# Layer 1 attention: gated outputs kept on chip in places that keys and weights leave, its pools in another order, and gate matmuls packed into the first head

## The chip, the cores and the metric

One core of one Trainium2 chip. The metric is device time in microseconds (us) of one execution of the whole program. The core has TensorE (PE in the profile, with PEld for its weight loads), VectorE (DVE), ScalarE (ACT), GpSimd (POOL) and SyncE (SP); in this kernel SP issues every DMA, in order.

## The reference

A trunk of two layers on x of 2048 tokens by 1024 features, float32. Layer 0 is windowed and chunked attention with a gate; the change leaves it alone. Layer 1 is differential attention with 8 heads of two 64-wide halves, causal by chunks of 64 tokens:

```python
q, k, v, gate = jnp.split(rms_norm(x, norm_g) @ w_in, [C_QK, 2 * C_QK, 2 * C_QK + C_W], axis=-1)
# per head: q1, q2 and k1, k2 are the normed, rotated halves
p1 = jax.nn.softmax(jnp.where(mask, s1, NEG_INF), axis=-1)
p2 = jax.nn.softmax(jnp.where(mask, s2, NEG_INF), axis=-1)
a = p1 - lam * p2
o = jnp.einsum('bhqk,bkhd->bqhd', a.astype(v.dtype), v)
o = rms_norm(o, subln_g) * (1.0 - lambda_init)
y = (o.reshape(b, s, C_W) * jax.nn.silu(gate)) @ w_out
return x + y
```

## The kernel before

All of it is float32, with operands split into a high and a low part (names ending in H and L), so that a product of the dense kind is three matmuls (`mm3`, L212 to L216: aH·bH, aH·bL, aL·bH). Call three such matmuls of 512 columns a unit.

Layer 0 and the projection of layer 1 (`project(1)`, which leaves q, k, v in DRAM) come first. The attention of layer 1 is `_mix1`. It goes over four blocks of 512 tokens from the last (b = 3) to the first (b = 0), and in each over 8 heads. A block b attends to b + 1 blocks of keys. Three streams are woven into one order by a function `pace`, when the program is built:

- **Scores** (`heads`, `scores`): for each head SP loads b + 1 blocks of keys (`load`, tiles k0 and k1, one for each half, tags with 4 buffers each; tiles vH and vL, 4 buffers each) and the queries (qd, ql, 2 buffers). For each of 4 rows of 128 tokens, each half and each 512 keys: two matmuls (L865, L866) into one of 4 PSUM banks, a maximum on DVE (L869) and an exponential on ACT (L872). Then POOL (every fifth time DVE) scales and adds the two halves (L893 to L899).
- **Values** (`values`): some way behind the scores (LAG1 units), the combined rows are transposed (L912), split (ACT L915, DVE L916) and multiplied with V (L919 to L921); then `gate` normalizes, multiplies with the gate g read back from DRAM, and its second half `rest` ends at L950 with the gated output o of one head and block.
- **Side work** (`side`): the gate projection (`gates`, 4 blocks of 64 units plus a store each 8, 288 steps), and then for each block the output projection (`projected`, 64 units plus 8 steps). Side units are what TensorE does where scores and values wait for the other engines.

How far the side work may be at each point is read from a table, `STAGES1`: pairs of (score units done, side steps done), with straight lines between. A head of block 3 has 58 score units, of block 2 42, of block 1 26, of block 0 10; in all there are 1088. What the table leaves at 1088 is done at the end, in the tail.

The output projection of a block needs the gated outputs of all eight heads as 16 tiles (yH and yL). Before, block 3's are split at once (`split`: ACT L967, POOL L968) and kept in pool `y` (16 buffers). Those of blocks 2 and 1 are stored to a DRAM tensor `o1` (L954), and `fetch` reads them back (tile oy, L978) and splits them when the projection of the block ahead is done, so that one set of 16 buffers serves three blocks in turn. Block 0's go into tiles that keys, values and weights no longer need (list `late`). `projected_last`, for block 0, takes weights for its second half from the places of the last queries and P1, and from k0 and k1.

Tiles share 4 buffers of tag `ot` among gate results, gated outputs, read-back outputs and residual rows.

## Time and profile before

| | us |
|---|---|
| time, median of 3 runs | 2954.62 |
| lowest and highest run | 2950.18, 2968.23 |
| the profiled execution, its own time | 2951.96 |
| span of the profiled execution | 2950.2 |
| mean granted clock of TensorE in it | 0.972 |
| PE, POOL, DVE, ACT busy over the span | 92%, 54%, 65%, 54% |

[...] A row of the view of waits says which engine and line waited for which, for how long in all, how often, and the longest. A row of the timeline gives start, duration, engine, line, operation and, in brackets, the wait ahead of it. The attention of layer 1 runs from about 1840 us to the end at 2950.2 us.

### The profile page before, as it was taken

How to read it: one execution, taken by the hardware profiler on the slowest of the kernel's cores; microseconds unless marked ns; L12 is line 12 of the kernel's file. 1: busy time of each engine (PE TensorE's matmuls, PEld its weight loads, DVE VectorE, ACT ScalarE, POOL GpSimd, SP SyncE). 2: the span in 40 equal slices, each digit the busy share in tenths (PEclk: the TensorE clock that was granted, in tenths of full speed). 3: DMA queues.
4: the chain of work that ended last, by engine and by line, in shares of the span. 5: the costliest groups of instructions: out<-in, count | busy, mean ns of one | idle time of the engine just before them, and what ended most of it. 6: DMA issues, size and time to landing. Idle time of an engine off the chain costs nothing.

```text
span 2950.2 us, 45159 instructions
## 1 busy us (share of the span) xinstructions
PE 2718.6 (92%) x13672; PEld 2242.1 (76%) x13672; DVE 1917.2 (65%) x4652; ACT 1593.5 (54%) x4135; POOL 1604.6 (54%) x1966
## 2 busy tenths in 40 slices
PE   6999999988888889899999998889999999899888
PEld 5888888876777788777788886667777777677667
DVE  7752385266677676498818861665766888878752
ACT  4443543367556565243334331666766777778752
POOL 3541251245345343267745650776777878789851
PEclk9999999999999999999999998999999999999999
DMA  4773343669988886475895455576768777668863
GB/s 149 230 250 120 113 147 120 197 192 249 262 214 212 216 217 170 146 270 197 259 302 191 127 162 158 164 217 197 225 193 234 200 225 214 176 169 243 221 215 114
DMA packets 427537, 580.79 MB, mean 197 GB/s; under 512 B 48160, under 2 KB 198688, under 8 KB 427296
## 3 DMA queue, kind: packets, MB, share of 16 engines
q1 hardware_dynamic: 427296, 577.92, 66.7%
q8 instruction: 109, 1.79, 0.3%
q14 instruction: 132, 1.08, 0.1%
HBM read 413.14 MB, written 164.63 MB: 196 GB/s over the span
## 4 chain that ended last, share of the span: by engine, by line
PE 63%; DMA 15%; DVE 11%; ACT 4%; POOL 3%; issue 3%; SPq 2%; DVEq 0%; ACTq 0%; POOLq 0%
PE p1mm L216 4%; PE p1mm L214 4%; PE p1mm L215 4%; PE p0mm L215 3%; PE p0mm L216 3%; PE p0mm L214 3%; PE cS L865 3%; PE ctr L912 3%; PE cS L866 3%; DMA mks<-bkL 2%; PE cO L920 2%; PE cG L214 2%; PE cG L216 2%; PE com L214 2%; DVE cnm L869 2%
## 5 line engine op out<-in xcount | busy, mean ns | idle before, releaser
L872 ACT ACTIVATE cP<-cS,cnm 128x512 f32<-128x512 f32 (+3 forms) x640 | 399.0, 630 | 173.8 <-DVE cnm L869 96.0
L869 DVE TENSOR_REDUCE cnm<-cS 128x1 f32<-128x512 f32 (+3 forms) x640 | 374.3, 600 | 100.6 <-PE cS L866 95.4
L865 PE MATMUL cS<-ck,cqd 128*128 128x512 f32 (+3 forms) x640 | 262.9, 415 | 60.0 <-ACT cP L872 20.5
L304 POOL TENSOR_TENSOR p0wL<-p0ws,p0wH 128x512 fp32r<-128x512 f32 (+1 forms) x128 | 155.3, 1246 | 276.0 <-ACT p0wH L303 266.4
L216 PE MATMUL p1mm<-p1wH,p1hL 128*128 128x512 f32 x768 | 303.3, 395 | 0.0
L215 PE MATMUL p1mm<-p1wL,p1hH 128*128 128x512 f32 x768 | 302.9, 395 | 0.4 <-POOL p1wL L304 0.4
L214 PE MATMUL p1mm<-p1wH,p1hH 128*128 128x512 f32 x768 | 302.3, 395 | 0.8 <-ACT p1wH L303 0.8
L899 POOL TENSOR_TENSOR cP<-cP,cP 128x512 f32<-128x512 f32 (+3 forms) x256 | 285.2, 1135 | 0.3
L304 POOL TENSOR_TENSOR p1wL<-p1ws,p1wH 128x512 fp32r<-128x512 f32 x128 | 168.0, 1333 | 136.8 <-ACT p1wH L303 97.5
L214 PE MATMUL p0mm<-p0wH,p0hH 128*128 128x512 f32 (+1 forms) x640 | 237.6, 374 | 3.5 <-ACT p0vt L454 2.6
L866 PE MATMUL cS<-ck,cql 128*128 128x512 f32 (+3 forms) x640 | 235.3, 372 | 3.3 <-DMA cql<-qL 3.3
L215 PE MATMUL p0mm<-p0wL,p0hH 128*128 128x512 f32 (+1 forms) x640 | 238.2, 373 | 0.0
L216 PE MATMUL p0mm<-p0wH,p0hL 128*128 128x512 f32 (+1 forms) x640 | 237.7, 372 | 0.1
L916 DVE TENSOR_TENSOR cptL<-ctr,cptH 128x512 fp32r<-128x512 f32 (+1 forms) x320 | 190.7, 599 | 62.4 <-ACT cptH L915 61.4
L865 PEld LDWEIGHTS cS<-ck,cqd 128*128 128x128 f32 x640 | 123.2, 193 | 104.4 <-ACT cP L872 51.2
L915 ACT ACTIVATE cptH<-ctr 128x512 fp32r<-128x512 f32 (+1 forms) x320 | 169.6, 539 | 58.2 <-PE ctr L912 57.0
L893 POOL TENSOR_SCALAR cP<-cP,ccs 128x512 f32<-128x512 f32 (+3 forms) x288 | 191.9, 683 | 0.0
L912 PE MATMUL ctr<-ident,cP 128*128 128x128 f32 x1088 | 175.4, 277 | 1.4 <-POOL cP L899 1.2
L898 POOL TENSOR_SCALAR cP<-cP,ccs 128x512 f32<-128x512 f32 (+3 forms) x256 | 174.0, 693 | 0.0
L214 PEld LDWEIGHTS p1mm<-p1wH,p1hH 128*128 128x128 f32 x768 | 145.3, 189 | 29.9 <-ACT p1wH L303 1.2
L215 PEld LDWEIGHTS p1mm<-p1wL,p1hH 128*128 128x128 f32 x768 | 145.2, 189 | 29.9 <-POOL p1wL L304 0.8
L216 PEld LDWEIGHTS p1mm<-p1wH,p1hL 128*128 128x128 f32 x768 | 145.4, 189 | 29.3 <-issue 0.2
(321 smaller groups left out, 7719.0 us busy)
## 6 DMA issues: line engine op xcount, KB each, us to landing
p1ws<-in_od_w_in_dram SPq DMA_DIRECT2D x56, 512.0 KB, 4.7
p0ws<-in_ev_w_in_dram SPq DMA_DIRECT2D x48, 512.0 KB, 4.3
ck<-kH SPq DMA_DIRECT2D x160, 128.0 KB, 4.0
ck<-kL SPq DMA_DIRECT2D x160, 128.0 KB, 4.2
cvH<-vH SPq DMA_DIRECT2D x80, 256.0 KB, 3.9
cvL<-vL SPq DMA_DIRECT2D x80, 256.0 KB, 4.7
cqd<-qH SPq DMA_DIRECT2D x128, 128.0 KB, 4.9
cql<-qL SPq DMA_DIRECT2D x128, 128.0 KB, 4.7
```

The source lines that it names most:

```text
L214: mm(ps, aH, bH, start=first, stop=False)
L215: mm(ps, aH, bL, start=False, stop=False)
L216: mm(ps, aL, bH, start=False, stop=last)
L304: nc.gpsimd.tensor_tensor(l[:, :width], ws[:, k, :width], f32(h[:, :width]), ALU.subtract)
L865: mm(ps, qd[:, m, js], kt[:, :wd], start=True, stop=False)
L866: self.anchor = mm(ps, ql[:, m, js], kt[:, :wd], start=False, stop=True).ins
L869: nc.vector.tensor_reduce(nm[:, m, z:z + 1], ps, AX.X, ALU.max, negate=True)
L872: nc.scalar.activation(chunks[z][:, :wd], ps, AF.Exp, bias=nm[:, m, z:z + 1], accum_out=acc)
L893: nc.gpsimd.tensor_scalar(p1, p1, c1, 1.0, ALU.mult, ALU.mult)
L899: nc.gpsimd.tensor_tensor(p1, p1, p2, ALU.add)
L912: nc.tensor.transpose(tp[:, (j - j0) * P:(j - j0 + 1) * P], us[j][kt // 4][:, kk:kk + P], self.ident)
L916: nc.vector.tensor_tensor(L[:, :wd], tp[:, :wd], f32(H[:, :wd]), ALU.subtract)
```

## The change

- The pools of `_mix1` are opened in another order, `ld` is parted into `w` (3 buffers) and `q` (2), P1 gets a pool of its own; sizes stay.
- `o1` is no longer written or read: L954's 16 stores and L978's 16 loads of 256 KB, and the 16 `ot` tiles that these loads filled, are gone. The split into yH and yL stands in `rest` for all blocks. Where the 16 tiles of each block lie is a table, `homes`: block 3 in `y`; block 2 in a key buffer of each half, a V buffer, the three weight buffers (heads 0 to 4) and then in `y` (heads 5 to 7); block 1 in `y` (heads 0 to 4), then a key buffer (head 5), a V buffer (head 6) and P0 (head 7); block 0 in `y`, key, V and weight buffers. So from head 0 of block 2 on, keys have three buffers for each half and not four until that place is free again.
- `STAGES1` has 45 side steps by score unit 32, where the line before reached 15; it is lower than before from about unit 400 on (288 steps at 640, where the line before had 304, and 490 at 1088, where it had 520; before, 16 of the steps were the read-backs of `fetch`).
- The projection of block 0 takes two P0 places for weights, not k0 and k1.

```diff
-    STAGES1 = ((0, 0), (600, 288), (780, 360), (1000, 440), (1088, 520))
+    STAGES1 = ((0, 0), (32, 45), (640, 288), (830, 360), (1035, 432), (1088, 490))
...
                 nc.vector.scalar_tensor_tensor(o, o, self.sub, sg, ALU.mult, ALU.mult)
-                if b in (0, NB - 1):
-                    split(h, b, o)
-                else:
-                    nc.sync.dma_start(s["o"][rows, tok], o)
-                ended.add((h, b))
+                yH, yL = y_tile(h, b), y_tile(h, b)
+                nc.scalar.activation(yH, o, AF.Copy)
+                nc.gpsimd.tensor_tensor(yL, o, f32(yH), ALU.subtract)
+                y[b][h] = yH, yL
...
-        def fetch(b):
-
-            for h in range(8):
-                while (h, b) not in ended:
-                    yield 0
-                if b < NB - 1:
-                    o = ot.tile([P, BLK], F32, tag="ot", name=n + "oy")
-                    nc.sync.dma_start(o, s["o"][h * P:(h + 1) * P, b * BLK:(b + 1) * BLK])
-                    split(h, b, o)
-                    yield 1
+        late = [(kp, "k0"), (kp, "k1"), (vp, "vH"), (vp, "vL")] + [(wp, "wH"), (wp, "wL")] * 3
+        homes = {
+            3: [(yp, "y")] * 16, 2: late + [(yp, "y")] * 6,
+            1: [(yp, "y")] * 10 + late[:4] + [(pp, "P0")] * 2, 0: [(yp, "y")] * 6 + late,
+        }
+
+        def y_tile(h, b):
+            pl, tag = homes[b].pop(0)
+            return pl.tile([P, BLK], F32R, tag=tag, name=n + "y" + tag)
...
             for b in (3, 2, 1):
-                yield from fetch(b)
+                while len(y[b]) < 8:
+                    yield 0
                 yield from projected(b)
             yield from projected_last()
```

The order of TensorE at the start of the first head (b = 3), in the program before; cS are scores, cG is the gate projection, and the rows follow one gate unit and eight score matmuls:

```order
L214 MATMUL cG<-p1hH,cwH 128x512
L215 MATMUL cG<-p1hL,cwH 128x512
L216 MATMUL cG<-p1hH,cwL 128x512
L865 MATMUL cS<-ck_21093,cqd 128x512
L866 MATMUL cS<-ck_21093,cql 128x512
```

The same place in the changed program, where the rows follow three gate units and the same eight score matmuls:

```order
L214 MATMUL cG<-p1hH,cwH 128x512
L215 MATMUL cG<-p1hL,cwH 128x512
L216 MATMUL cG<-p1hH,cwL 128x512
L867 MATMUL cS<-ck_21099,cqd 128x512
L868 MATMUL cS<-ck_21099,cql 128x512
L214 MATMUL cG<-p1hH,cwH 128x512
L215 MATMUL cG<-p1hL,cwH 128x512
L867 MATMUL cS<-ck_21109,cqd 128x512
L868 MATMUL cS<-ck_21109,cql 128x512
L216 MATMUL cG<-p1hH,cwL 128x512
```

Four gate units stand ahead of the fifth score where there were two. Over the whole first head, counted from its first score matmul to the next head's, the order holds 13 gate units before and 37 now; heads 1 to 7 of block 3 had 171 and now have 147.

The order of TensorE in head 5 of block 0 in the program before, the last two rows of scores of that head (com is the output projection):

```order
L865 MATMUL cS<-ck_34546,cqd 128x384
L866 MATMUL cS<-ck_34546,cql 128x384
L865 MATMUL cS<-ck_34549,cqd 128x384
L866 MATMUL cS<-ck_34549,cql 128x384
L865 MATMUL cS<-ck_34546,cqd 128x512
L866 MATMUL cS<-ck_34546,cql 128x512
L865 MATMUL cS<-ck_34549,cqd 128x512
L866 MATMUL cS<-ck_34549,cql 128x512
L919 MATMUL cO<-cptH,cvH 128x512
```

The changed program, scores of the same size one head earlier in the same block:

```order
L867 MATMUL cS<-ck_34422,cqd 128x384
L868 MATMUL cS<-ck_34422,cql 128x384
L214 MATMUL com<-p1hH,cyy 128x512
L215 MATMUL com<-p1hL,cyy 128x512
L216 MATMUL com<-p1hH,cyy 128x512
L867 MATMUL cS<-ck_34419,cqd 128x512
L868 MATMUL cS<-ck_34419,cql 128x512
L214 MATMUL com<-p1hH,cyy 128x512
L215 MATMUL com<-p1hL,cyy 128x512
L216 MATMUL com<-p1hH,cyy 128x512
L214 MATMUL com<-p1hH,cyk_33264 128x512
L215 MATMUL com<-p1hL,cyk_33264 128x512
```

Output units that stood behind the last scores stand between them now; cyy and cyk are y tiles in pool `y` and in a key buffer. Output units per head of block 0, heads 0 to 7: 1, 0, 1, 3, 3, 0, 41, 80 before, and 5, 4, 4, 6, 10, 8, 11, 93 now.

SP's order in block 2 before, where the keys of head 5 (ck_28984, ck_28994) are issued and the first keys of head 6 (ck_29484, ck_29487) stand among them:

```order
L989 DMA ck_28984<-kH 64x512
L990 DMA ck_28984<-kL 64x512
L989 DMA ck_29484<-kH 64x512
L989 DMA ck_28994<-kH 64x512
L990 DMA ck_28994<-kL 64x512
L990 DMA ck_29484<-kL 64x512
L989 DMA ck_29487<-kH 64x512
L990 DMA ck_29487<-kL 64x512
```

SP's order in the changed program where the first keys of head 6 of block 2 (ck_29431, ck_29434) are issued:

```order
L984 DMA cvL<-vL 128x4x128
L977 DMA ck_29431<-kH 64x512
L978 DMA ck_29431<-kL 64x512
L977 DMA ck_29441<-kH 64x512
L978 DMA ck_29441<-kL 64x512
L977 DMA ck_29451<-kH 64x512
L977 DMA ck_29434<-kH 64x512
L978 DMA ck_29434<-kL 64x512
L977 DMA ck_29444<-kH 64x512
L978 DMA ck_29444<-kL 64x512
```

The first block of keys of a head was loaded a whole head ahead, into the fourth buffer; now all three blocks of head 6 are loaded one after another where head 5 ends.

## Rows read from the trace of the kernel before

**Rows 1.** Stretches: window, its length, busy us of each engine, clock, DMA, GB/s.
```profile
core 0: us, PE busy (x) PEld busy (x) DVE busy (x) ACT busy (x) POOL busy (x), PEclk, DMA share, GB/s
1840.50:1846.00 5.50, 5.34 (x13) 4.08 (x14) 2.29 (x5) 2.36 (x8) 0.00 (x0) 0.50 0.98 298
...
1840.50:1875.50 35.00, 30.17 (x107) 20.32 (x107) 22.27 (x53) 22.47 (x68) 18.01 (x27) 0.87 0.53 162
1875.50:2248.40 372.90, 347.51 (x1697) 276.83 (x1698) 244.89 (x534) 249.19 (x677) 275.04 (x365) 0.98 0.70 200
2248.40:2550.80 302.40, 288.90 (x1441) 230.27 (x1440) 245.83 (x525) 216.67 (x605) 239.28 (x330) 0.99 0.75 215
2550.80:2816.00 265.20, 233.24 (x1141) 183.69 (x1139) 212.38 (x581) 199.64 (x586) 229.62 (x344) 0.94 0.78 210
2816.00:2830.00 14.00, 10.42 (x51) 7.30 (x50) 9.63 (x29) 10.54 (x30) 13.29 (x21) 1.00 0.86 233
2816.00:2950.20 134.20, 120.75 (x549) 94.55 (x547) 45.51 (x102) 51.31 (x116) 46.15 (x58) 0.97 0.51 161
```

**Rows 2.** Waits of PE, 1826 to 2951 us: total, times, longest.
```profile
PE cO L920 <- DVE cptL L916: 21.8, 23, 3.7
PE cS L865 <- ACT cP L872: 20.5, 37, 2.2
PE cS L865 <- DMA cqd<-qH: 18.2, 3, 13.4
PE cS L865 <- DMA ck<-kL: 17.3, 5, 7.9
PE com L214 <- ACT cyP L967: 3.7, 1, 3.7
```

**Rows 3.** Timeline of PE, matmuls one behind another in block 3.
```profile
2129.91 0.39 PE L214 MATMUL cG<-p1hH,cwH 128*128 128x512 f32 x1
...
2130.59 0.39 PE L920 MATMUL cO<-cptL,cvH 128*128 128x512 f32 x1
...
2131.05 0.60 PE L912 MATMUL ctr<-ident,cP 128*128 128x128 f32 x4
2131.41 0.47 PE L919 MATMUL cO<-cptH,cvH 128*128 128x512 f32 x1
```

**Rows 4.** Instructions of line 968 (POOL's part of a split), by what they read.
```profile
L968 POOL TENSOR_TENSOR cy<-coy,cy x16: 1260/1280/1297, 2573.3 to 2817.4; 128x512 fp32r<-128x512 f32 x16
L968 POOL TENSOR_TENSOR cy<-cot,cy x8: 1274/1284/1296, 1959.7 to 2323.8; 128x512 fp32r<-128x512 f32 x8
```

**Rows 5.** Timeline of PE, waits at the starts of heads 3 and 6 of block 3.
```profile
1991.08 0.79 PE L865 MATMUL cS<-ck,cqd 128*128 128x512 f32 x1 [7.86 <-DMA ck<-kL]
...
2149.84 0.39 PE L865 MATMUL cS<-ck,cqd 128*128 128x128 f32 x1 [2.87 <-DMA ck<-kL]
```

**Rows 6.** DMA issues, 1826 to 2951 us: queue, count, KB each, median us to landing.
```profile
ck<-kL SPq DMA_DIRECT2D x152, 128.0 KB, 4.3
...
cwL<-wgL SPq DMA_DIRECT2D x64, 256.0 KB, 4.9
...
o<-cot SPq DMA_DIRECT2D x16, 256.0 KB, 3.6
coy<-o SPq DMA_DIRECT2D x16, 256.0 KB, 5.0
```

**Rows 7.** Timeline of PE about its last long wait.
```profile
2913.86 1.02 PE L946 MATMUL cms<-csq,ones 128*128 128x512 f32 x2
2918.55 0.79 PE L214 MATMUL com<-p1hH,cyP 128*128 128x512 f32 x1 [3.67 <-ACT cyP L967]
```

**Rows 8.** Stretches behind that wait, columns as in Rows 1.
```profile
2918.50:2925.00 6.50, 6.45 (x16) 5.01 (x17) 2.20 (x4) 0.00 (x1) 1.28 (x1) 0.52 0.21 77
2925.00:2935.00 10.00, 10.00 (x46) 8.25 (x45) 0.28 (x1) 0.00 (x0) 0.00 (x0) 1.00 0.59 186
```

More of the change, by code (lines that the diff above doesn't have):

```diff
@@ L817, in _mix1 @@
         pool = lambda nm, bufs, **kw: es.enter_context(tc.tile_pool(name=n + nm, bufs=bufs, **kw))
-        ot = pool("ot", 4)
-        sm = pool("sm", 8)
-        ld = pool("ld", 2)
         yp = pool("y", 2 * KT)
         vp = pool("v", 4)
+        ot = pool("ot", 4)
+        wp = pool("w", 3)
+        sb = pool("sb", 3)
+        sm = pool("sm", 8)
+        qp = pool("q", 2)
+        kp = pool("kp", 4)
+        pq = pool("p2", 6)
         pp = pool("pp", 19)
-        kp = pool("kp", 4)
-        sb = pool("sb", 2)
         NS, NTR, NO, NM = self.BANKS1
@@ L840, in scores @@
             tok = slice(b * BLK, (b + 1) * BLK)
-            qd = ld.tile([P, 2, BLK], F32R, tag="qd", name=n + "qd")
-            ql = ld.tile([P, 2, BLK], F32R, tag="ql", name=n + "ql")
+            qd = qp.tile([P, 2, BLK], F32R, tag="qd", name=n + "qd")
+            ql = qp.tile([P, 2, BLK], F32R, tag="ql", name=n + "ql")
             for m in range(2):
@@ L869, in scores @@
                         nc.vector.tensor_reduce(nm[:, m, z:z + 1], ps, AX.X, ALU.max, negate=True)
-                        chunks.append((sb if m else pp).tile([P, 512], F32, tag=f"P{m}", name=n + f"P{m}", bufs=6 if m else None))
+                        chunks.append((pq if m else pp).tile([P, 512], F32, tag=f"P{m}", name=n + f"P{m}"))
                         acc = la[:, m, z:z + 1] if nb > 1 else l[:, m:m + 1]
@@ L912, in values @@
                     nc.tensor.transpose(tp[:, (j - j0) * P:(j - j0 + 1) * P], us[j][kt // 4][:, kk:kk + P], self.ident)
-                H = sb.tile([P, 512], F32R, tag="ptH", name=n + "ptH", bufs=3)
-                L = sb.tile([P, 512], F32R, tag="ptL", name=n + "ptL", bufs=3)
+                H = sb.tile([P, 512], F32R, tag="ptH", name=n + "ptH")
+                L = sb.tile([P, 512], F32R, tag="ptL", name=n + "ptL")
                 nc.scalar.activation(H[:, :wd], tp[:, :wd], AF.Copy)
@@ L932, in gate @@
             rows, tok = slice(h * P, (h + 1) * P), slice(b * BLK, (b + 1) * BLK)
-            g = sb.tile([P, BLK], F32, tag="g", name=n + "gg")
+            g = sb.tile([P, BLK], F32, tag="g", name=n + "gg", bufs=2)
             nc.sync.dma_start(g, s["g"][rows, tok])
@@ L1002, in _mix1 @@
         room = self.last_hidden
-        ended = set()
-        late = [(ld, "wH"), (ld, "wL")] * 3 + [(kp, "k0"), (kp, "k1"), (vp, "vH"), (vp, "vL")] * 2 + [(pp, "P0")] * 2
         def load_w(c, k, to):
@@ L1019, in gates @@
                             for part in "HL":
-                                t = ld.tile([P, 4, P], F32R, tag="w" + part, name=n + "w" + part, bufs=3)
+                                t = wp.tile([P, 4, P], F32R, tag="w" + part, name=n + "w" + part)
                                 nc.sync.dma_start(f32(t), s["wg" + part][c, :, k:k + 4, :])
@@ L1070, in projected_last @@
             w = [(room[0][:, k, :], room[1][:, k, :]) for k in range(KT)], []
-            tags = [(ld, "qd"), (ld, "ql")] * 2, [(sb, "P1")] * 6 + [(kp, "k0"), (kp, "k1")]
+            tags = [(qp, "qd"), (qp, "ql")] * 2, [(pq, "P1")] * 6 + [(pp, "P0")] * 2
             pairs = []
@@ L1077, in projected_last @@
                 pairs.append([
-                    pl.tile([P, BLK], F32R, tag=tag, name=n + "w" + tag, bufs=6 if tag == "P1" else None)
+                    pl.tile([P, BLK], F32R, tag=tag, name=n + "w" + tag)
                     for pl, tag in tags[1][2 * i:2 * i + 2]
@@ L1085, in projected_last @@
                 for k in range(KT):
-                    while (k, 0) not in ended:
+                    while k not in y[0]:
                         yield 0
```

10 lines of the change are left out of this document (removed).

## The prediction

> **What bounds the kernel now.** I read the stretches first, then the waits of TensorE (PE), then the timeline at single waits. The change touches only layer 1's attention, from 1840.5 us, the first score matmul, to 2950.2; the windows are cut where the first score of a head starts.
>
> To put times on moved work I counted every TensorE instruction of each head in the built orders, from its first score to the next head's, and priced them by width. A 512-column matmul takes 0.227 us where nothing holds it up (2129.91 to 2130.59 is three, [rows 3]), so a unit takes 0.68; narrower ones go in proportion, and four transposes take 0.36 to 0.44, since the matmul behind them starts slowly. The work (us), before and now:
>
> - block 3, head 0: 22.5, now 38.9; heads 1 to 7: 322.0, now 306.3
> - block 2: 266.4, now 255.9
> - block 1 and heads 0 to 5 of block 0: 192.7, now 220.9
> - the tail, heads 6 and 7 of block 0 to the end: 106.2, now 87.7
>
> The sums are the same, 909.8 and 909.7: the change moves work and takes none from TensorE. So a gain can only come from the 200 us in which it has none to do, and the stretches [rows 1] show where these lie. Time per work is 35.0/22.5 = 1.56 in head 0, 372.9/322.0 = 1.16 in the rest of block 3, 302.4/266.4 = 1.14 in block 2, 265.2/192.7 = 1.38 in block 1 and six heads of block 0, and 134.2/106.2 = 1.26 in the tail. Blocks 3 and 2 are TensorE's. From 2550.8 to 2816 POOL is the busiest for its pace: 229.62 of 265.2 us (87%), and 13.29 of the next 14; there scores wait for the combining of rows, and the side work that could fill the gaps is held back. The output projections of blocks 2 and 1 must first read their outputs from DRAM (5.0 us a load, behind a store of 3.6 [rows 6]), and six heads of those 14 have no output unit or one. What was not done there is done in the tail.
>
> **The change part by part**, against the profiled execution (2951.96; the median is 2.7 higher).
>
> *A. Gates into head 0 of block 3.* 24 more units (16.4 us) come into a stretch that has 12.5 us without work. At the pace of the other heads 38.9 x 1.16 = 45, so +10. Below it is +3.9 (all the idle time taken), above +16.4 (none). Heads 1 to 7 lose 15.7 of work, at 1.16: -18; if softmax sets their pace as much as TensorE, -12. Their side work is still 17 to 24 units a head. Net **-8**, from -14 to +4. The 13.4 us wait for the first queries [rows 2] stays: the first 40 DMAs stand in the same order.
>
> *B. Block 2.* 10.5 us less work at 1.14 is -12. Two things are given back. Head 4 has 2 gate units where the others have 14 to 19, since the next weights need a place that an output of block 2 holds now; the last are issued right before their use, and such a load lands after 4.9 us [rows 6]: +5. And keys have three buffers for three blocks. From head 3 on (five heads) all blocks of the next head are loaded when this one has read its own, with 5 to 10 us of work between a buffer's last use and its next, where the first block had about 40. A load lands in 4.3 us [rows 6] and is issued 1 to 3 us after the release. The price of a head start lies between 0 and the longest such wait of block 3, where four buffers serve four blocks: 7.86 [rows 5]. I take 1 us, as the slack is about the landing plus the issue: +5. Net **-2**, from -12 to +10.
>
> *C. Block 1 and six heads of block 0.* Before, all 16 splits of blocks 2 and 1 ran on POOL between 2573.3 and 2817.4, 1.28 us each [rows 4]. Block 2's eight now run in block 2, where POOL is busy 239.28 of 302.4 us and covers them. POOL has 10.2 us less here: 219.4 at 87% is 253, -12. The 28.2 us more work for TensorE is to fit under it: 220.9/253 = 0.87, the share of block 2 (266.4/302.4 = 0.88). If that cover were gone it would cost up to 28.2. The key loads of eight heads are as short here (4.4 to 7.5 us), but scores run ahead of POOL and a wait of a microsecond is mostly hidden: +2. The 32 DMAs of 256 KB are gone and help the queries' loads; I give them nothing, since other loads stay ahead of those in SP's order. Net **-10**, from -15 to +16.
>
> *D. Tail.* 18.5 us of output units have been done before: -18.5, since behind 2830 nothing but TensorE paces [rows 1]; at 1.26 it would be -23. The last gate chain makes TensorE wait 3.67 us [rows 7], as its outputs are needed right behind its matmul cms; now 5.5 us of other output units stand between: -3.7. [...] Net **-25**, from -15 to -30. Splits of the last block cost the same as before.
>
> Pool order, the queries' own pool and the other places for the last weights move no instruction of their own that I find on a path: 0.
>
> Sum: -8 -2 -10 -25 = -45, 2907 on the profile's level, **2910** on the median's. All times below are on that level.
>
> **The clock.** In part C's stretch the clock is 0.94, in block 2 it is 0.99 [rows 1]. With two levels, 0.94 means 12% of 265.2 us, 32 us, at the lower one, where 16 us of full-rate work was done. The rows at 1840.5 (0.50 behind the wait of 13.4) and 2918.5 show it low behind waits [rows 1, 2, 8]. If filling the gaps gives all of that back and POOL lets it count, 16 us more are gained.
> [...]
>
> **The rivals.**
>
> 1. *The added units lengthen part C one for one.* TensorE takes its instructions in order, so a unit ahead of a score makes the score, and POOL behind it, late. For it: scores wait only 20.5 us in all for their banks [rows 2], in many short pieces. Against it: POOL has work queued, as scores run 36 units ahead. Then C is 28.2 - 12 = +16 and not -10: 2936.
> 2. *Lost key prefetch eats it, the case on the other side.* 13 head starts (block 2 from head 3, block 1) stand as block 3's do, of which 5 of 7 waited, 17.3 us together [rows 2]. At 2.87 each [rows 5] it is 37 us, 30 more than I took: 2940. It eats the whole gain at (45 + 7)/13 = 4.0 each, and is over 1% slower at 6.3; at 7.86 it is 3005. For it: two DMAs a tile through one in-order queue. Against it: block 3's waits came where the last block's load was issued late, some 6 us after the release, and these are not.
> 3. *Head 0 becomes bound by its loads.* 24 units bring 12 weight loads and 3 stores, 3.9 MB, to the 5.7 MB that it moved (35.0 us at 162 GB/s): 9.6 MB in 45 us is 213 GB/s, and the queue was full at 298 GB/s in its first 5.5 us [rows 1]. With A's upper +16.4 and one wait of 7.86 behind it: 14 us lost, 2924.
> 4. *The change does not do what it says*: the tiles of blocks 2 and 1 wait for their borrowed places, and ACT, in order, with them, so that exponentials behind them come late. 16 such splits at a wait like 2.87 are 46 us: 2956.
> 5. *The clock comes back* as well: 2894.
>
> **How the numbers follow.** Forecast 0.55, its own range 2892 to 2928; rival 1 0.19; 2 0.06; 3 0.06; 4 0.08; 5 0.06. A measurement of this kernel can tell about 1% (under 2925, over 2984) from no change. Faster: the forecast, the clock, half of rival 3 and a part of rival 1, 0.65. Within 1%: the rest of 1 and 3, rival 4 and a third of 2, 0.29. Slower: rival 2 with long waits and a mishap in the placing, 0.06. The range 2885 to 2945 takes in rivals 1, 3 and 5 and the milder 2; rival 4, the longer 2 and the ends of the forecast, some 0.18, lie outside.
>
> **What would show each step.** A: head 0 near 45 us and heads 1 to 7 near 355. B: block 2 near 300, with waits for key tiles near 1 us at its head starts, and one of about 5 for gate weights in head 4. C: block 1's start to head 6 of block 0 near 255, POOL about 219 busy, the clock over 0.94. D: from there to the end near 109, with no wait of 3.7 for the last tiles and no stretch at 0.52 behind it. I am wrong if key waits in blocks 2 and 1 come to over 30 us, if POOL's pace in C falls as TensorE fills, or if splits hold up ACT.

## The result, and the profile after

| | before | changed |
|---|---|---|
| median of 15 runs, us | 2959.7 | 2973.1 |
| lowest and highest | 2950.2, 2974.7 | 2963.4, 2984.3 |
| profiled execution, own time | 2951.96 | 2984.29 |
| its span | 2950.2 | 2982.5 |

The changed kernel takes 1.0035 times the time of before (95% interval 1.0018 to 1.0052): about 10 us more (13 by the medians), where the prediction had 45 less. The two profiled executions are 32 us apart, since one was among the fastest of its kernel (8 us under its median) and the other its slowest; a second profile of the changed kernel (run `again`, below) lies at 2966.57. From the first score on, the profiles show 1109.7 us before and 1139.8 and 1131.7 us now, 30 and 22 more, where the times differ by about 10: so the losses by stretch below are too large by some us each, and what both profiles show weighs more than what one shows.

The stretches of the changed kernel's first profile, cut where [rows 1] cut those of before (window and length, busy us of PE, PEld, DVE, ACT, POOL, each with its number of instructions, then the granted clock of TensorE, 1.00 being the full one, the busy share of the DMA engines, GB/s): head 0 of block 3, heads 1 to 7, block 2, block 1 with heads 0 to 5 of block 0, the tail.

```profile
1842.70:1889.20 46.50, 43.20 (x179) 34.62 (x180) 23.64 (x53) 25.77 (x74) 24.83 (x37) 0.93 0.71 206
1889.20:2266.30 377.10, 342.60 (x1631) 273.37 (x1630) 250.18 (x536) 247.10 (x673) 269.90 (x359) 0.95 0.65 187
2266.30:2586.80 320.50, 291.90 (x1396) 230.56 (x1394) 239.61 (x523) 218.29 (x611) 241.26 (x333) 0.95 0.69 193
2586.80:2875.40 288.60, 256.62 (x1288) 204.83 (x1286) 231.26 (x600) 212.37 (x611) 234.06 (x353) 0.97 0.69 185
2875.40:2982.50 107.10, 97.28 (x444) 78.45 (x441) 34.75 (x84) 34.70 (x81) 30.37 (x43) 0.97 0.54 175
```

The same stretches of its second profile:

```profile
1833.10:1878.30 45.20, 43.54 (x180) 35.06 (x181) 23.80 (x53) 25.77 (x74) 24.91 (x37) 0.90 0.69 212
1878.30:2250.60 372.30, 340.45 (x1630) 271.02 (x1629) 247.56 (x536) 247.27 (x673) 270.89 (x359) 0.96 0.64 190
2250.60:2565.20 314.60, 285.40 (x1396) 226.00 (x1394) 240.09 (x523) 218.28 (x611) 241.69 (x332) 0.97 0.69 197
2565.20:2858.10 292.90, 260.78 (x1288) 208.53 (x1286) 226.66 (x600) 212.17 (x611) 236.27 (x354) 0.95 0.64 182
2858.10:2964.80 106.70, 97.16 (x443) 78.38 (x441) 34.75 (x84) 34.79 (x81) 30.39 (x43) 0.97 0.54 176
```

| us | before [rows 1] | predicted | first profile | second profile |
|---|---|---|---|---|
| head 0 of block 3 | 35.0 | 45 | 46.5 | 45.2 |
| its heads 1 to 7 | 372.9 | 355 | 377.1 | 372.3 |
| block 2 | 302.4 | 300 | 320.5 | 314.6 |
| block 1, heads 0 to 5 of block 0 | 265.2 | 255 | 288.6 | 292.9 |
| tail | 134.2 | 109 | 107.1 | 106.7 |

Head 0 and the tail came near the forecast. The 27 us that the tail gave were lost again: heads 1 to 7 of block 3 gave nothing for 16 us less work, block 2 took 12 to 18 us more for 10 us less work, and the stretch behind it 23 to 28 us more, where 10 less was expected.

Two windows of the first profile hold most of the last two losses: heads 4 and 5 of block 2, and head 7 of block 1.

```profile
2417.60:2511.90 94.30, 81.02 (x376) 63.11 (x375) 63.34 (x136) 57.62 (x160) 59.55 (x83) 0.91 0.61 172
2758.00:2801.40 43.40, 35.49 (x172) 27.60 (x171) 33.40 (x74) 29.99 (x82) 34.50 (x50) 0.92 0.57 154
```

The same heads in the kernel before:

```profile
2407.40:2476.70 69.30, 66.59 (x337) 52.68 (x335) 64.77 (x131) 49.90 (x144) 57.00 (x79) 1.00 0.79 233
2723.80:2745.30 21.50, 20.25 (x103) 16.09 (x102) 19.29 (x48) 17.05 (x52) 18.30 (x29) 1.00 0.74 191
```

Heads 4 and 5 went from 69.3 to 94.3 us, with 67.6 us of TensorE work now and 61.6 before. Head 7 of block 1 went from 21.5 to 43.4, with 27.8 us of work and 18.4. In both the clock was 1.00 before and is 0.91 to 0.92 now.

The waits of TensorE in the attention of the changed kernel's first profile (what waited for what: us in all, times, longest), to stand beside [rows 2]:

```profile
PE cS L867 <- DMA ck<-kL: 24.5, 10, 5.7
PE cO L922 <- DVE cptL L918: 22.6, 24, 3.8
PE cS L867 <- ACT cP L874: 22.0, 29, 3.2
PE cS L867 <- DMA cqd<-qH: 14.2, 2, 12.9
PE cG L214 <- DMA cwH<-wgH: 11.6, 6, 3.8
PE com L214 <- DVE cxr L1036: 3.6, 2, 3.1
```

New are the 11.6 us for gate weights (11.8 in the second profile); the waits for keys grew by 7 us only (9 in the second profile). The wait for the last tiles is gone, as forecast. A new one stands earlier in the tail, where head 7 of block 0 waits for its keys (4.0 us in the second profile), and the clock is 0.53 over the 6.4 us behind it:

```profile
2901.67 0.44 PE L867 MATMUL cS<-ck,cqd 128*128 128x128 f32 x1 [4.36 <-DMA ck<-kL]
...
2901.60:2908.00 6.40, 6.33 (x20) 5.34 (x20) 2.48 (x12) 2.54 (x9) 1.98 (x4) 0.53 0.91 294
```

### The profile page after: what moved, and what is told of

Same layout as the page of the kernel before. It is cut to its first block, busy times and chain, and to the rows that moved or that the text cites. A ratio compares the mean times of both kernels' runs of the same rounds, so it can differ in the third digit from the quotient of the medians.

```text
span 2982.5 us, 45078 instructions
## 1 busy us (share of the span) xinstructions
PE 2731.6 (92%) x13672; PEld 2260.0 (76%) x13672; DVE 1927.5 (65%) x4652; ACT 1589.7 (53%) x4135; POOL 1597.2 (54%) x1966
## 4 chain that ended last, share of the span: by engine, by line
PE 66%; DMA 13%; DVE 8%; ACT 3%; issue 2%; POOL 2%; SPq 1%; ACTq 0%; DVEq 0%; POOLq 0%
PE p1mm L214 5%; PE p1mm L215 5%; PE p1mm L216 5%; PE cS L867 3%; PE cS L868 3%; PE ctr L914 3%; PE p0mm L216 3%; PE p0mm L214 3%; PE p0mm L215 3%; PE cO L922 2%; PE com L214 2%; PE com L215 2%; PE com L216 2%; PE cG L214 2%; DMA ck<-kL 2%
## 5 line engine op out<-in xcount | busy, mean ns | idle before, releaser
L215 PE MATMUL p1mm<-p1wL,p1hH 128*128 128x512 f32 x768 | 302.4, 394 | 0.4 <-POOL p1wL L304 0.4
L887 POOL TENSOR_SCALAR ccs<-ce,crl 128x4 f32<-128x4 f32 (+2 forms) x96 | 27.0, 282 | 261.9 <-DVE crl L884 187.3
```

Source lines behind the costliest of these rows:

```text
L215: mm(ps, aH, bL, start=False, stop=False)
```

## The experiments

Ratios are to the kernel before on the same chip, with their 95% intervals. All kernels have the same TensorE work in the attention, within 1 us, so a stretch is given as time/work in us, the work priced as in the prediction. Stretches come from one profile of each kernel, and the same order of TensorE doesn't always take the same time: heads 1 to 7 of block 3 with the old table and no dense head, 322 us of work, took 372.9 us in the kernel before and 376.2, 379.0 and 380.3 in the runs oldtable, keyslost and kf_old; block 2 in the changed kernel's order took 320.5, 314.6 and, in kf_b1, 313.7. A difference of 7 us between two profiles shows nothing by itself.

**The changed kernel again.**

> The changed kernel once more, for a second profile. Theory T (table): the new table of shares costs the time, by waits for gate weights and keys in block 3 and by the thin head 4 of block 2. Theory P (places): the borrowed key and V places cost it, at the head starts of blocks 2 and 1. Theory C (clock by chance): the first profile (2984) was a run in which the clock fell more often than usual, and the stretches that lost in it are not those that lose in another. All expect a median near 2973. T and P expect the same stretches to lose as in the first profile: heads 1 to 7 of block 3 near 377 us at a clock near 0.95, block 2 near 320, head 7 of block 1 near 43. C expects at least one of these to be back at the value of before (373, 302, 21).

Median 2965.68, ratio 1.0025 (1.0007 to 1.0043). Block 2 and head 7 of block 1 (44.1 us) lose as in the first profile, so these losses are not chance. Heads 1 to 7 are back at the 372 to 373 us of before, which theory C named as its sign: the 377 of the first profile was in part chance. What both profiles lack is the gain of 18 us. TensorE's clock over heads 1 to 7 was 0.95 and 0.96, over block 2 0.95 and 0.97.

**The two halves apart.** The old table under the new places, and the new table in the kernel before:

```diff
-    STAGES1 = ((0, 0), (32, 45), (640, 288), (830, 360), (1035, 432), (1088, 490))
+    STAGES1 = ((0, 0), (600, 288), (780, 360), (1000, 432), (1088, 504))
```

> The changed kernel with the table of before, less the 16 steps of reading back: (600, 288), (780, 360), (1000, 432), (1088, 504). Outputs stay on chip in the same places. T expects it to be under before's 2960, near 2945, since the places cost little and the 32 transfers are gone. P expects it at 2970 or more, as the places are the same, with waits at the head starts of blocks 2 and 1. The thin head 4 of block 2 (2 gate units) becomes one with 15 output units here, as the gates end before the weight places are borrowed; block 3 stands as before, so its heads 1 to 7 should take 373 us by T and by P.

```diff
-    STAGES1 = ((0, 0), (600, 288), (780, 360), (1000, 440), (1088, 520))
+    STAGES1 = ((0, 0), (32, 45), (640, 288), (830, 360), (1035, 440), (1088, 506))
```

> The kernel before with the new table (the steps of reading back added: 440 at 1035, 506 at 1088); outputs go through DRAM as before, keys keep their places. T expects 2970 or more: head 0 of block 3 near 46, heads 1 to 7 near 377. P expects about 2960 or less: the stretches of block 3 change as predicted (45 and 355) and block 2 stays near 300.

oldtable: 2956.79, ratio 0.9985 (0.9970 to 1.0000). newtable: 2969.25, 1.0021 (1.0001 to 1.0041). The table costs in both settings, which theory T expected and P did not; but oldtable is only 4 us under before, not 15, so the places cost too, as P had it, if less than P's 2970 or more. In newtable, heads 1 to 7 of block 3 take 373.3/306.3, the time of before for 16 us less work, with no borrowed place in the program. T expected 377 there. Head 0 takes 44.1 us, 9 more than before; most of the rest of newtable's loss is in its tail, where this table leaves more to do and the changed kernel is fast:

```profile
2822.20:2971.00 148.80, 127.20 (x564) 99.30 (x563) 51.08 (x105) 55.11 (x123) 51.32 (x64) 0.94 0.50 160
```

148.8 us against 134.2 before. So newtable's loss is not the changed kernel's loss in block 2 and behind it.

**Keys free.** Outputs that lay in key buffers go to two P0 places (buffers of the first half's exponentials); in a further run only those of block 1:

```diff
-            3: [(yp, "y")] * 16, 2: late + [(yp, "y")] * 6,
-            1: [(yp, "y")] * 10 + late[:4] + [(pp, "P0")] * 2, 0: [(yp, "y")] * 6 + late,
+            3: [(yp, "y")] * 16, 2: [(pp, "P0")] * 2 + late[2:] + [(yp, "y")] * 6,
+            1: [(yp, "y")] * 10 + [(pp, "P0")] * 2 + late[2:4] + [(pp, "P0")] * 2, 0: [(yp, "y")] * 6 + late,
```

> The changed kernel with the outputs that lay in key places (head 0 of block 2, head 5 of block 1) in two P0 places instead, so that keys keep four buffers for each half. Head 4 of block 2 has 9 gate units then, not 2, and head 7 of block 1 20.3 us of work, not 27.8. P expects 15 to 25 us less than the changed kernel, 2950 to 2958, with block 2 near 303 and head 7 of block 1 near 22. T expects it within 8 us of the changed kernel, with block 2 still near 315.

> The changed kernel with P0 places only for block 1's head 5; head 0 of block 2 lies in key places again, so keys have three buffers through block 2 and four in block 1 from its head 5 on. The order of block 2 is that of the changed kernel, head 4 with 2 gate units and all; head 7 of block 1 has 19 us of work, not 28. If the cost lies where head 7 of block 1 stood at 43 us, this is near the kernel with keys free (2951 to 2955) and block 2 stays at 314 to 320. If it lies in block 2, it is 2962 or more.

keysfree: 2950.59, ratio 0.9974 (0.9959 to 0.9989), some 15 us under the changed kernel on the same chip. kf_b1: 2958.21, 0.9999 (0.9982 to 1.0017), so block 1's place makes up about 9 us of them. Head 7 of block 1 is the window where it shows, here in keysfree:

```profile
2734.70:2758.30 23.60, 22.43 (x124) 18.29 (x122) 21.36 (x59) 18.01 (x54) 22.65 (x35) 1.00 0.66 186
```

From 43.4 to 23.6 us (in kf_b1 23.8), with the clock back at 1.00. Head 0 of block 0 behind it grows from 10.7 to 18.1, since work that the order had drawn ahead of its scores goes back there; the stretch as a whole falls from 289 and 293 to 273 us, in kf_b1 to 277. Block 2 is at 307 us in keysfree and at 314 in kf_b1, where its order is still that of the changed kernel.

**The key places alone**, in the kernel before: two key buffers are taken at head 0 of block 2 and held, unused, until block 0.

```diff
+                    if (b, h) == (2, 0):
+                        held[:] = [kp.tile([P, BLK], F32R, tag=f"k{m}", name=n + f"held{m}") for m in range(2)]
+                        for t in held:
+                            nc.vector.memset(f32(t)[:, 0:1], 0.0)
...
+                if (b, h, kt) == (0, 1, 0):
+                    for t in held:
+                        nc.vector.tensor_tensor(small("hold"), f32(H[:, 0:1]), f32(t)[:, 0:1], ALU.mult)
```

> The kernel before with one key buffer of each half held, unused, from head 0 of block 2 to head 1 of block 0, so that only the key places are lost; outputs go through DRAM, table and order of TensorE as before (head 3 to 5 of block 2 move by a microsecond of work each). Two tiny instructions on VectorE write what is held and two read it. Theory L (the lost places cost by themselves): 10 to 16 us over the kernel before, by waits for key tiles at the head starts of blocks 2 and 1. Theory O (the price comes from the order that the builder makes of late keys, as in head 7 of block 1 of the changed kernel, whose work grew from 18 to 28 us): within 5 us of before, since the order hardly moves here.

2972.40, ratio 1.0050 (1.0032 to 1.0068): 15 us, theory L's size with an order that hardly moved. But not by waits of the kind that L named. TensorE's waits from block 2 to head 5 of block 0 in this run:

```profile
PE cO L923 <- DVE cptL L916: 18.8, 17, 3.3
PE cS L865 <- ACT cP L872: 12.4, 18, 3.2
PE cS L865 <- DMA ck<-kL: 4.8, 3, 3.9
```

Those for keys are 4.8 us. What grew is a wait of SP, which issues all loads in order. SP's longest waits in the same stretch, of this run (line 992 loads keys, 999 loads V; before, these are lines 989 and 996):

```profile
SPq L992 <- PE cS L866: 50.5, 24, 8.9
SPq L999 <- PE cO L924: 39.4, 19, 9.4
```

and of the kernel before:

```profile
SPq L996 <- PE cO L921: 38.3, 15, 7.7
SPq L989 <- PE cS L866: 21.1, 17, 2.9
```

SP stands 50.5 us at key loads that wait for a score to have read a buffer out, up to 8.9 us at a time, where it stood 21.1; loads behind them in the queue wait with them. (In the trace of the kernel before, SP's longest wait of block 2, 7.7 us for a buffer of V, shows how: SP issues nothing from 2488.6 to 2496.3 us, and then the V loads at 2496.26 and 2496.71 and the residual row behind them at 2497.22.) All rows of the key loads' line together, whatever is waited for, come to 69.7 us here and 49.8 before. But this wait does not price the loss: keysfree has 74.7 us of it and kf_old (below) 69.2, and both are faster than the kernel before. How the 15 us come about stays open.

**Is block 3 paced by TensorE's work?** Half its gates are moved to block 2, in the kernel before:

```diff
-    STAGES1 = ((0, 0), (600, 288), (780, 360), (1000, 440), (1088, 520))
+    STAGES1 = ((0, 0), (464, 110), (660, 288), (800, 360), (1000, 440), (1088, 520))
```

> The kernel before with a table that leaves block 3 about half its gate units (7 in head 0, 12 or 13 in each of heads 1 to 7; the rest goes to block 2). Heads 1 to 7 of block 3 then hold 265 us of TensorE work, where before has 322 and the changed kernel 306 at 373 and 372 to 377 us. If something else than TensorE's work paces these heads (theory F, a floor), they take 355 us or more. If TensorE paces them at 1.16 of its work, as the prediction had it (theory W), they take 307. The whole time is not at stake: block 2 gets long.

Heads 1 to 7 of block 3:

```profile
1874.10:2229.80 355.70, 311.48 (x1448) 240.14 (x1448) 252.74 (x542) 243.90 (x672) 274.56 (x365) 0.92 0.54 159
```

355.7/264.8, at the edge of what F expected: 57 us less work gave 17 us (up to 25 by the other three profiles of the old order), where 1.16 a unit of work would have given 66. In its place stand other waits: for banks that ACT has to read (cS <- ACT cP) 25.6 us where before has 4.7, for POOL's combined rows 7.9 where before has 1.2, and the clock went from 0.98 to 0.92. (The run's one time is 2987.6, as the gates crowd block 2.) What sets the floor is not shown: no other engine is busy for more than 78% of the stretch, and how much of it is the lower clock was not tried.

**The dense head.** Out of the keys-free kernel, and into the kernel before with its own table:

```diff
-    STAGES1 = ((0, 0), (32, 45), (640, 288), (830, 360), (1035, 432), (1088, 490))
+    STAGES1 = ((0, 0), (640, 288), (830, 360), (1035, 432), (1088, 490))
```

> The kernel with keys free (outputs of head 0 of block 2 and head 5 of block 1 in P0 places) and the new table without its step at 32, so head 0 of block 3 has 13 gate units again. F expects head 0 back at 35 us and heads 1 to 7 at 373, though they hold 10 us more work: 8 us less than with keys free, 2943. W expects heads 1 to 7 to take 12 us more, and the whole to stay at 2951 or rise.

```diff
-    STAGES1 = ((0, 0), (600, 288), (780, 360), (1000, 440), (1088, 520))
+    STAGES1 = ((0, 0), (32, 45), (600, 288), (780, 360), (1000, 440), (1088, 520))
```

> The kernel before with only the step (32, 45) put into its own table. As above: 2950 to 2960 if the dense head is worth something or nothing by itself, 2965 or more if it costs. Heads 1 to 7 of block 3 hold 312 us of work, between the 322 of before and the 306 of the changed kernel, which took the same 373; head 0 near 44. If they again take 373, the whole is 9 us longer there and the 24 units are saved only where gates end, in block 2, 7 us less work.

kf_nodense: 2964.68, ratio 1.0015 (0.9996 to 1.0034), 14 us over keysfree. F was wrong here: head 0 is back at 36.8, but heads 1 to 7 take 388.3/316.5 and block 2 317.2/263.2 (in a profile that was the slowest of its kernel, 10 us over the median). b_dense: 2956.89, 1.0000 (0.9985 to 1.0014), with 42.3 in head 0 and 365.4/311.9 in heads 1 to 7. So the dense head costs nothing in the one setting and saves 12 to 14 us in the other. It does not explain the loss. Why the thinner order of kf_nodense is so slow in heads 5 and 6 (58.9 and 61.8 us) is open.

**Keys free with the old table**, without and with the dense head:

```diff
-    STAGES1 = ((0, 0), (32, 45), (640, 288), (830, 360), (1035, 432), (1088, 490))
+    STAGES1 = ((0, 0), (600, 288), (780, 360), (1000, 432), (1088, 504))
```

> Keys free, and the table of before less the steps of reading back: the on-chip outputs alone, with neither the key places nor the new table. If the price of the key places and that of the table add up (16 us and 9 to 13 us by the runs so far), it is near 2940, 20 us under the kernel before. If they are two names for one thing (key loads late in a tight order), it stays at 2950 or above. Block 2 should be near 303 and the stretch to head 5 of block 0 near 275.

```diff
+    STAGES1 = ((0, 0), (32, 45), (600, 288), (780, 360), (1000, 432), (1088, 504))
```

> Keys free and the table of before less the read-backs, with the step at 32 added: 45 side steps by unit 32, then on to 288 at 600. Against the run with keys free and the old table (2944): if the dense head pays only together with a thinner block 3, as the runs with the new table with and without it say (2951 and 2965), this is 2935 to 2944. If the whole new table is dearer and the dense head has a part in it, 2945 to 2955. Head 0 of block 3 should be near 44 and heads 1 to 7 between 365 and 375.

kf_old: 2944.47, ratio 0.9958 (0.9938 to 0.9977); kf_dense_old: 2951.08, 0.9976 (0.9962 to 0.9990), where 2935 to 2944 was expected if the dense head pays; it is the other case, 2945 to 2955, though the two intervals overlap. Outputs on chip, with the new order of the pools, are worth about 12 us when no key place is given away; the key places leave 4 of them (oldtable). So the key places cost 8 us under the old table and 15 under the new (keysfree), and the table 5 us with keys free and 12 with key places (oldtable against `again`). The prices grow when the two come together, by some 7 us; the intervals leave open whether that is more than chance.

**Gates ended earlier.** One number of the changed kernel, with the key places left borrowed:

```diff
-    STAGES1 = ((0, 0), (32, 45), (640, 288), (830, 360), (1035, 432), (1088, 490))
+    STAGES1 = ((0, 0), (32, 45), (560, 288), (830, 360), (1035, 432), (1088, 490))
```

> The changed kernel with its gates ended at score unit 560 and not 640 (dense head and later points kept, key places borrowed as in it). Block 2's head 4 then has 10 output units and not 2 gate units, head 5 has 9 and not 26, and no weight for gates is loaded into places that outputs hold; block 3 gets 6.6 us and more of work per head back (321 us in heads 1 to 7), block 2 244 and not 256. If the thin head 4 and the crowded head 5 are what block 2 lost beyond the key places (heads 4 and 5 took 94 and 91 us for 68 us of work), block 2 comes to 290 to 297 and the whole to 2955 to 2962. If the key places are all of it, block 2 loses only its 12 us of work at 1.14 and stands at 302 or more, and the whole stays at 2966 or more.

2941.96, ratio 0.9944 (0.9921 to 0.9968): some 25 us under the changed kernel, more than either case expected. Heads 1 to 7 of block 3, block 2, block 1 with heads 0 to 5 of block 0, and in it head 7 of block 1:

```profile
1886.40:2257.80 371.40, 348.46 (x1697) 281.81 (x1696) 249.24 (x536) 249.21 (x676) 271.52 (x359) 0.96 0.72 212
2257.80:2540.90 283.10, 265.90 (x1338) 211.34 (x1337) 243.73 (x522) 214.84 (x606) 240.56 (x325) 0.99 0.68 192
2540.90:2836.40 295.50, 259.65 (x1277) 206.34 (x1276) 238.92 (x600) 213.32 (x612) 237.36 (x360) 0.95 0.64 179
...
2719.80:2764.60 44.80, 36.77 (x174) 29.43 (x172) 35.88 (x76) 29.73 (x81) 35.06 (x49) 0.85 0.51 145
```

Block 3's heads 1 to 7 hold 321.3 us of work again, 15 more than in the changed kernel, and take 371.4 us, no longer. Block 2 falls from 315 and 320 to 283.1/243.4 us; 18 to 22 us of the fall lie in heads 4 and 5, which take 72.5 us together. The key place of block 1 still costs: head 7 is at 44.8.

**Both cures, and where they belong.** Gates ended at 560 or 500, with keys free in both blocks (kf_) or in block 1 alone (kb1_):

> Gates ended at unit 560 and keys free, both: head 0 of block 2 and head 5 of block 1 in P0 places. If the price of the key places (16 us by the changed kernel with and without them) and that of the late gates (25 to 30 us) are two things, this is 15 us under the run with gates ended at 560 (2942): 2922 to 2932, with head 7 of block 1 near 22 and not 45. If ending the gates early already frees the queue and the buffers so that keys come in time, it stays at 2938 or above, apart from what head 7 of block 1 shows.

> As the other, with the gates ended at unit 500: heads 1 to 7 of block 3 hold 333 us of work and not 321, block 2 235 and not 246. Heads 1 to 7 took 371 to 377 us for anything from 306 to 322 us of work. If the floor reaches to 333, they take 375 or less and the whole gains up to 10 us more on the other run; if TensorE's work paces from here on, they take 12 us more, 383 or more, and the whole is the same or 5 us worse.

> Gates ended at unit 560, outputs of block 2's head 0 in key places as in the changed kernel, those of block 1's head 5 in P0 places. With gates ended at 560, block 2 took 283 us with key places and 296 with P0 places; the stretch from block 1 to head 5 of block 0 took 295 with key places and 284 with P0. If each block's price goes with its own places, this has the better of both, 283 and 277 to 284, and is 10 to 15 us under gates560: 2927 to 2932. If one run's stretches traded time with the next by chance, it stays at 2942.

> The same places, gates ended at unit 500. With P0 places in block 2 that kernel stood at 2937, its block 2 at 300 us for 235 us of work, its block 3 at 377 for 333. If P0 places are what held its block 2 at 300, block 2 falls to 275 to 285 here and the whole to 2920 to 2928. If block 2 has a floor of its own near 295, it stays near 2937.

| | median | ratio (95%) | block 3, heads 1 to 7 | block 2 | block 1 to head 5 of block 0 |
|---|---|---|---|---|---|
| kf_gates560 | 2944.19 | 0.9948 (0.9930 to 0.9966) | 366.5/321.3 | 295.7/245.7 | 283.8/215.4 |
| kf_gates500 | 2937.24 | 0.9934 (0.9910 to 0.9959) | 376.7/333.0 | 299.8/235.1 | 269.8/214.2 |
| kb1_gates560 | 2930.82 | 0.9901 (0.9866 to 0.9936) | 365.1/321.3 | 285.7/243.4 | 284.5/217.7 |
| kb1_gates500 | 2937.07 | 0.9933 (0.9909 to 0.9956) | 372.6/333.0 | 291.7/235.0 | 271.0/214.4 |

kf_gates560 missed its 2922 to 2932; kb1_gates560 came as expected. With gates ended at 560, block 2 takes 295.7 us with its output in P0 places and 283.1 and 285.7 with it in key places; in block 1 it is the other way round. So kf_gates560 gave back in block 2 what it won in block 1, and kb1_gates560, which has the better place in each, is the best kernel of the study: 1% under the kernel before, 28 us by the medians. With gates ended at 500 the two kernels are equal by their medians, where 2920 to 2928 was expected of kb1_gates500, though block 2's stretch is 8 us shorter in its profile; so the price of P0 places in block 2 is shown for one table only. Its block 2, block 1 to head 5 of block 0, and head 7 of block 1:

```profile
2247.60:2533.40 285.80, 269.79 (x1339) 215.16 (x1338) 244.94 (x522) 214.93 (x606) 241.39 (x329) 0.98 0.66 191
2533.40:2817.80 284.40, 255.59 (x1270) 201.47 (x1269) 231.38 (x598) 210.79 (x608) 236.46 (x356) 0.97 0.67 187
...
2710.30:2732.90 22.60, 21.38 (x112) 17.00 (x111) 20.33 (x57) 18.53 (x55) 20.96 (x31) 1.00 0.68 185
```

The floor of block 3 holds for 333 us of work as well (372.6 and 376.7). Block 2 may have one too: with 8 us less work, kb1_gates500's takes 6 us more, and kf_gates500's, with 11 us less, 4 us more than kf_gates560's; but such differences are within what two profiles differ by.

## Why the prediction was wrong, by its own steps

*The opening premise held*: the change moves work and takes none away. From it followed that a gain must come out of idle time. What was missed is that the idle time of a stretch does not shrink with its work. Three terms failed by it or beside it: heads 1 to 7 in A, then B and C, together -30 us in the forecast, where the stretches of the two profiles show +46 and +39 (too large by some us, as the profile of before was a fast one).

*A, head 0*: right, +10 to +11 for +10. *A, heads 1 to 7*: this step failed. It took 1.16 us of time for each us of work as a price that also holds when work is taken out. It is an average, not a slope. Heads 1 to 7 took 372 to 377 us for 306 us of work in all five profiles with that order (two of the changed kernel, newtable, keysfree, kf_b1), and in kb1_gates500 372.6 for 333; from 322 down to 265 the slope is 17/57 = 0.30, or 0.43 from the slowest profile of the old order. Time follows work so little here that kf_nodense, with 316.5 us of it, is the longest of all. The term was -18 and measured -1 (second profile) to +4, or some -3 by the means of these five profiles (374) and of the four of the old order (377). The other pace, that of softmax, was named as a bound (-12) and was not a bound at all: the upper end of the term should have been no gain.

*B*: the sign failed. Forecast -2, measured +12 to +18, and +11 in kf_b1, which has the same block 2. The price of the weights' places was put at one late load of 5 us, and that of the keys at 1 us a head start. The profile has such waits (3.2 us for gate weights at the end of head 4, and no more than 1.4 us for keys in all of block 2). But the two together made the order itself bad: head 4 with 2 gate units, head 5 with 26 units behind it. In the kernel before with the new table (late gates, no borrowed places) block 2 takes 300.6/254.7; with the old table and places borrowed (oldtable) 306.6/266.6; in the changed kernel with gates ended early, places borrowed, 283.1/243.4. Late gates together with borrowed places give 314 to 321, and 307.5 and 317 where the key places are spared but those of weights are not (keysfree, kf_nodense). The order was read, and head 4's 2 units were seen; the mistake was to price them by one wait. Head 4 in the changed kernel, and in the kernel before, where it has 15 output units:

```profile
2417.60:2461.50 43.90, 32.75 (x143) 24.06 (x142) 34.77 (x67) 28.64 (x81) 35.55 (x50) 0.87 0.48 121
...
2407.40:2441.90 34.50, 33.93 (x174) 26.98 (x172) 32.71 (x67) 25.04 (x73) 27.64 (x38) 1.00 0.66 189
```

24.1 us of work take 43.9 us, and before 31.3 took 34.5. The head lost 11.2 us in waits that the profile names (5.3 for DVE's split, 3.2 for gate weights, 2.2 for banks), and the clock is low for part of it. It has two levels in the traces: in the kernel before it is 0.50 from 2918.5 to 2924.5 us, with 0.43 us from one matmul of 512 columns to the next, and 1.00 from 2925.5, with 0.23. By these a mean of 0.87 is 11 us at the lower level, some 6 us lost. Why a head with less work is slower, and not only as slow as softmax lets it be, is open; kf_b1's head 4, in the same order, takes 43.9 us too.

*C*: failed most, -10 forecast, +23 to +28 measured. Three parts:
- The key place of block 1's head 5. It was priced with the head starts, at 2 us; it costs 9 to 13 us (kf_b1 against the changed kernel, kb1_gates560 against gates560), the whole of it in head 7 (20 us), less 8 us that head 0 of block 0 gives back. Head 7's 27.8 us of work stood in the list of the order and was taken for work like any other. It is values drawn ahead of block 0's first scores (kf_b1 has 9 us less work in head 7 and 5 more in head 0). TensorE waits there for DVE, 6.3 us in the first profile and 6.5 in the second, at a mean clock of 0.92 and 0.88; that late keys make the builder draw it ahead is argued from the order.
- POOL was to lose 10.2 us of splits. It lost none: 14 splits lie in the stretch now and 15 did before, since block 2's last heads and block 0's first have theirs in it too; POOL is busy 234 to 236 us there, 229.6 before. And its pace fell, which the prediction had named as a sign that it is wrong: busy for 81% of the stretch in both profiles, where it was 87%. With keys free it is 86% again (234.4 of 272.9 us in keysfree).
- The added units were taken to be hidden. With keys free they cost 8 to 12 us for 26 to 28 us of work (keysfree and kf_b1 against before): neither nothing nor the one for one of rival 1. Rival 1's premise is in the trace: in head 5 of block 0 before, the last eight score matmuls and the value matmul behind them start in the built order, from 2807.68 to 2813.52 us, and behind the wait of 2.18 us for a bank among them none starts ahead of its turn. By POOL's 5 us more, at 87%, keysfree's stretch would be 269 us of its 273, so in it POOL's pace still covers nearly all of the work; that is an estimate, not a test.

*D*: the total was right, 107.1 and 106.7 for 109, in part by luck. The step of 3.7 us came as forecast: output units between the last cms and its first use cover it, and no stretch at 0.52 follows there. The other 3.1 us of the -25 stand for the clock behind the old wait, 0.52 over 6.5 us [rows 8]. No run shows that term by itself: the clock is 1.00 behind the last cms now, but a wait of 4.4 us for the keys of head 7 came, with 6.4 us at a clock of 0.53 behind it (shown above), and the tail's mean clock is 0.97 as before. What the two small terms won at the last cms, this wait took back; the 9 us gained besides the 18.5 of moved work came from other idle time of the tail, which the sum had not counted. Behind the last cms, in the first profile:

```profile
2945.00:2955.00 10.00, 10.00 (x44) 7.94 (x43) 2.13 (x3) 1.95 (x3) 1.28 (x1) 1.00 0.17 60
```

*The clock* neither came back, as rival 5 had it, nor stayed as it was. In C it rose from 0.94 to 0.95 and 0.97, but in heads 1 to 7 it fell from 0.98 to 0.95 and 0.96, in block 2 from 0.99 to 0.95 and 0.97. By the two levels, a mean lower by 0.03 is 6% more of 377 us at the lower one: 23 us, in which at most 11 us of work was not done. That may be part of why heads 1 to 7 gained nothing; it was not tried, and two profiles of the old order (oldtable, kf_old) stand at 0.96 as well.

*The rivals.* The second, lost key prefetch, was given 0.06 and is the nearest to what happened: keyslost puts it at 15 us by itself, twice the 7 that stood in the sum. Its own description was off: the named waits for keys are few (1.4 us in block 2 and 9 behind it, in the second profile), and it would not have decided alone: 8 us more for keys leave 37 of the 45. Of the others, rival 3 is out, as head 0 came near its 45 us, and rival 4 too: ACT's splits waited 5.2 us in all in the changed kernel, for DVE's results, and not for places. That A and B erred the same way is one error twice: both priced the idle time of a stretch as if it stood in proportion to TensorE's work. C went by POOL's pace, and erred on what POOL has to do and on the pace itself.

Measured apart, 12 us are gained by outputs on chip (kf_old), 15 lost by key places (keyslost) and 6 by the table (newtable): +9, and +10 was measured. That they agree is partly chance, as the table loses in newtable's tail and not where the changed kernel loses, and the key places cost 8 us and not 15 under the old table; with 8 and the table's 5 (keysfree against kf_old) the sum is +1. Ending the gates at 560 takes away 25 us, more than the table costs in the kernel before. The new order of the pools alone was not run; it is part of the 12 us.

## What to carry to other kernels

The ratio of a stretch's time to an engine's work is no price for work moved in or out: ask what paces the stretch when that work is gone, and give the term no gain as one end of its range. Filler work belongs where the main stream has a floor of its own (here block 3, whose gates cost nothing up to 333 us of work), and taking it out of there frees little time. When a transfer is saved by borrowing the place of a prefetch buffer, read the new order for heads whose filler vanishes or whose later work is drawn ahead, and price those heads whole; which place is lent matters per stage: the key place was dear in block 1 and, with gates ended at 560, cheaper than a P0 place in block 2.

## What the runs showed of the hardware that was not expected

The attention started anywhere from 1833 to 1851 us in profiles of programs that are the same up to there, so some 18 us of a run's time are settled before the stretch that a change touches. Durations of a stretch are the better measure than its ends.

A VectorE instruction on 4 to 8 elements a partition takes 0.17 us at the median and up to 5.07 in the changed kernel (and 3.96 in the kernel before). The longest stands in the chain of work inside the thin head 4:

```profile
L882 DVE TENSOR_TENSOR cpe<-ce,cla x96: 140/167/5073, 1858.5 to 2784.6; 128x8 f32<-128x8 f32 x32, 128x6 f32<-128x6 f32 x32, 128x4 f32<-128x4 f32 x32
```

The longest one, and what POOL did as it ended:

```profile
2440.05 5.07 DVE L882 TENSOR_TENSOR cpe<-ce,cla 128x6 f32<-128x6 f32 x1
...
2440.99 2.89 POOL L901 TENSOR_TENSOR cP<-cP,cP 128x512 f32<-128x512 f32 x3
2443.84 1.26 POOL L944 TENSOR_TENSOR cot<-cot,cgg 128x512 f32<-128x512 f32 x1
```

It ends at 2445.1 us, where a run of POOL's instructions without a gap ends. The three longest of the kernel before (3.96, 3.78 and 3.47 us, ending at 2412.98, 2316.39 and 2456.67) end within 0.03 us of such a run's end too. That POOL holds it was not tried.
